# Short projections of a hybrid decoder's recurrence: float32 multiplications replaced by pairs of float32r multiplications on split rows

## The chip, the cores and the metric

One core of one Trainium2 chip runs the whole program. The metric is the device time of one launch in microseconds (us); less is better.

## The reference, cut to what matters

One layer of a decoder is computed for 264 columns: 256 tokens of a prompt and one new token for each of 8 decoded sequences. Its parts are a feed-forward half step, a mixer, an attention over 256 memory tokens and a second half step. The mixer has a recurrence of 16 heads of 64 and a convolution beside it; the lines that the change touches compute this part of the recurrence:

```python
r, k, v, wd, ad, gd = jnp.split(pm, SPLITS, axis=-1)       # pm: shifted projections
w_log = -softplus(-(w0 + tanh(wd) @ w2_decay)) - 0.5        # wd: 64 columns
decay = exp(-exp(w_log))
a = sigmoid(a0 + ad @ a2_iclr)                              # ad: 64 columns
g = sigmoid(gd) @ g2_gate                                   # gd: 160 columns
kk = (k * k_k).reshape(B, T, 16, 64)
kk = kk / maximum(norm(kk, axis=-1), 1e-12)                 # a sum by head
...                                                         # recurrence -> y
bonus = sum(r * k * r_k, axis=-1) * v                       # a sum by head
o_a = (group_norm(y) + bonus) * g                           # two more sums by head
merged = concat([o_a * beta_rwkv, o_b * beta_conv]) @ w_out
```

## The kernel before, in words

**Tiling.** Activations lie with features on partitions and the 264 columns along the free axis. Each large weight matrix comes from memory in tiles of 128 by 1024 (raw, 512 KB). ScalarE copies a tile to float32r (whi, L188), VectorE computes the rest (wlo, L189), and TensorE makes three float32r multiplications for each block: high weight by high activation, high by low, low by high (L303 to L305, result acc). This stream of tiles runs through the whole program. The loads stand in SyncE's queue (L266).

**The recurrence.** Its 8 blocks of 128 features are worked in four groups of two (groups 0 to 3), while the projections of the mixer stream: MIX_ORDER (L40) names which projection follows which, and generators (rw_state, rw_read, rw_out, with the decode rows and the convolution) are stepped in between. What a generator yields is a pace; the tile scheduler then sets each engine's order from its own costs. `lora` (L704) makes the short activations: wdad (64 rows of tanh(wd), 64 of ad) and sga, sgb (sigmoid(gd)). `rw_state` (L719) does for each group: loads the short weights w2a2 and g2 (L727 to L736, half filled with zeros by GpSimd), the squares of k (L746), two multiplications for the decay (pw, L749), two for a (pa, L761), the scan (L766), two sums of squares by head against the block of ones blk (ps, L772), Ln and Exp, and the operands ar, bk and q. The rows q for decode (L811 to L813) are transposed by TensorE (L1010). Then come the gram matrices (L886 on TensorE, G by L890 on VectorE), transposes of bk (L825), and the inversion of small triangles, which alternates TensorE (L843, L850) and VectorE (L835, L836, L851, L852). I call this the gram stretch. `rw_read` (L963) has the sum for the bonus (L977), `rw_out` (L1078) the two sums for the group norm (L1087, L1093) and the gate's multiplications (L1104, L1105), each with two per block.

**The end of the mixer.** `mixer_out` (L1274) splits the 16 blocks of the result into xh and xl (L189) and `out_proj` (L1206) multiplies them by w_out, beginning with block 0 in four accumulators; its first low part, xl of block 0, is a VectorE instruction.

Of the kernel before, what the change touches and what calls it, by code (L numbers as in the profile page):

```python
# [8 lines left out]
F32 = mybir.dt.float32  # L9
F32R = mybir.dt.float32r  # L10
# [11 lines left out]
T = TP + TB  # L22
# [31 lines left out]
class Builder:  # L54
# [553 lines left out]
    def mixer_consts(self):  # L608
# [23 lines left out]

        self.blk = self.ct([128, 128], "blk")
        nc.vector.memset(self.blk, 0.0)
        for o in HS:
            nc.vector.memset(self.blk[o, o], 1.0)

# [65 lines left out]

    def lora(self, P):  # L704
        nc = self.nc
        xh, xl = self.xs
        self.wdad, self.sga, self.sgb = (self.mt(n) for n in ("wdad", "sga", "sgb"))
        ((a0, a1),) = yield from self.gemm(P[0], xh, xl)
        self.shift(a0, 24, self.wdad)
        self.fn(self.wdad[0:64], self.wdad[0:64], AF.Tanh)  # L710
        self.shift(a1, 25, self.sga)
        self.fn(self.sga, self.sga, AF.Sigmoid)
        ((b0,),) = yield from self.gemm(P[1], xh, xl)
        self.shift(b0, 26, self.sgb)
        self.fn(self.sgb[96:128], self.sgb[96:128], AF.Sigmoid)


    def rw_state(self, g, S):
# [7 lines left out]

        w2a2, g2 = self.mt("w2a2", (128, 2, 256), bufs=2), self.mt("g2", (128, 2, 256), bufs=2)  # L727
        for n, o in enumerate(HS):
            nc.gpsimd.memset(w2a2[o, 1 - n], 0.0)
        nc.gpsimd.memset(g2[0:96, 1], 0.0)  # L730
        gs = slice(256 * g, 256 * g + 256)
        nc.sync.dma_start(w2a2[0:64, 0], self.I["w2_decay"][0][:, gs])
        nc.sync.dma_start(w2a2[64:128, 1], self.I["a2_iclr"][0][:, gs])
        nc.sync.dma_start(g2[:, 0], self.I["g2_gate"][0][0:128, gs])
        nc.sync.dma_start(g2[96:128, 1], self.I["g2_gate"][0][128:160, gs])
        S["g2"] = g2  # L736
        c8 = lambda t: t[:, :, :TP].rearrange("p i (c t) -> p i c t", t=C)
# [5 lines left out]
        a = S["a"] = self.mt("a", G3)  # L743
        t1, t2 = self.mt("t1", G3), self.mt("t2", G3)
        for i, j in enumerate(js):
            A.activation(t1[:, i], k[:, i], AF.Square, scale=self.mcol("k_k", j))  # L746
        pw = [self.misc() for _ in js]
        for i, j in enumerate(js):
            mm(pw[i][:, :T], w2a2[:, 0, cs[i]], self.wdad, start=True, stop=True)  # L749
        for i, j in enumerate(js):  # L750
# [9 lines left out]
        for i, j in enumerate(js):  # L760
            mm(pa[i][:, :T], w2a2[:, 1, cs[i]], self.wdad, start=True, stop=True)  # L761
        for i, j in enumerate(js):
            self.fn(a[:, i], pa[i][:, :T], AF.Sigmoid, bias=self.mcol("a0", j))
        L = self.mt("L", (128, NP, C + 1))
        fl = lambda t: t.rearrange("p c t -> p (c t)")
        V.tensor_tensor_scan(fl(L), fl(self.rst), fl(sig), 0.0, ALU.mult, ALU.add)  # L766
        Lc = sig
# [3 lines left out]
        for i, j in enumerate(js):  # L771
            mm(ps[i][:, :T], self.blk, t1[:, i], start=True, stop=True)  # L772
        for i, j in enumerate(js):
# [191 lines left out]
    def rw_read(self, g, S):  # L965
# [6 lines left out]
        for i, j in enumerate(js):  # L972
            V.scalar_tensor_tensor(r[:, i], r[:, i], self.mcol("r_k", j), k[:, i], ALU.mult, ALU.mult)
        yield 1.0
        for i, j in enumerate(js):
            p = self.misc()
            mm(p[:, :T], self.blk, r[:, i], start=True, stop=True)  # L977
            V.tensor_tensor(v[:, i], p[:, :T], v[:, i], ALU.mult)
# [25 lines left out]
    def decode_rows(self, g, S):  # L1004

        nc = self.nc
        q = S["q"]
        n = 5 * 2 * TB
        ps = self.misc()
        nc.tensor.transpose(ps[:n, :128], q[:, 0:5].rearrange("p q i b -> p (q i b)"), self.ident)  # L1010
        row = self.mt("row", (n, 128))
        nc.scalar.activation(row, ps[:n, :128], AF.Copy)
        self.rows[g] = scr = self.dram.tile([10, 2, TB, C], F32, tag="row", name=self.uid("scr"), bufs=4)
        for h in range(2):
            nc.scalar.dma_start(
                scr[:, h], row[:, C * h : C * h + C]
            )
# [61 lines left out]
    def rw_out(self, g, S):  # L1079
        nc = self.nc  # L1080
        V, A = nc.vector, nc.scalar
        mm = nc.tensor.matmul
        y, t1, t2, bon, g2 = S["y"], S["k"], S["r"], S["v"], S["g2"]
        js = (2 * g, 2 * g + 1)
        for i in range(2):
            p = self.misc()
            mm(p[:, :T], self.blk, y[:, i], start=True, stop=True)  # L1087
            V.scalar_tensor_tensor(y[:, i], p[:, :T], -1.0 / C, y[:, i], ALU.mult, ALU.add)
# [12 lines left out]
        for i, j in enumerate(js):  # L1101
            cs = slice(128 * i, 128 * i + 128)
            p = self.misc()
            mm(p[:, :T], g2[:, 0, cs], self.sga, start=True, stop=False)  # L1104
            mm(p[:, :T], g2[:, 1, cs], self.sgb, start=False, stop=True)  # L1105
            V.scalar_tensor_tensor(self.oa[j], y[:, i], self.mcol("beta_rwkv", j), p[:, :T], ALU.mult, ALU.mult)
# [144 lines left out]
    def mixer(self, pool, P):  # L1251
# [5 lines left out]
        self.last = self.mt("last", (128, 27, TB + 1))  # L1257
        self.rst = self.mt("rst", (128, NP, C + 1))
        nc.gpsimd.memset(self.rst, 1.0)
# [614 lines left out]
```

## Time and profile before

| | |
|---|---|
| median of 3 runs | 2525.59 us (2519.16 to 2527.02) |
| the profiled execution | 2526.33 us, of which the span is 2524.6 us |
| granted TensorE clock, mean | 0.993 |
| TensorE busy | 2470.9 us, 98% |
| VectorE busy | 1582.8 us, 63% |
| ScalarE busy | 1195.0 us, 47% |
| GpSimd busy | 261.7 us, 10% |

TensorE has work nearly all the time over the span. The shares are means over stages that differ: in the stretch of the recurrence VectorE's share is much higher than its 63%. Starts are counted from the start of the span. Matmuls overlap, so the distance from one start to the next says what one takes, not its length.

### The profile page before, as it was taken

To read this page: it belongs to the slowest core of one execution; us is meant where nothing else is said; L and a number is where in the kernel's file an instruction comes from. 1 tells how busy PE (TensorE), PEld (TensorE's weight loads), DVE (VectorE), ACT (ScalarE), POOL (GpSimd) and SP (SyncE) were. 2 spreads that over 40 slices of the span, in tenths; PEclk is the share of its full clock that TensorE was granted. 3 is DMA by queue.
4 is the path that set the end of the run, shared out by engine and by line. 5 is a ranking of instruction groups with operands and counts; after the bars stand their busy time and mean duration, and the time that the engine had idled before them with its cause. 6 is when DMAs were issued, how large, how long until landed. Compare 5 with 4: busy or idle time off the path is not lost. (4 is left out here: it accounts for less than half of the span.)

```text
span 2524.6 us, 53420 instructions
## 1 busy us (share of the span) xinstructions
PE 2470.9 (98%) x22328; PEld 2417.2 (96%) x22328; DVE 1582.8 (63%) x2545; ACT 1195.0 (47%) x1802; POOL 261.7 (10%) x422
## 2 busy tenths in 40 slices
PE   9999999999999999999989999999999999999998
PEld 9999999999999988988889888989999999999998
DVE  5545444444557599799777566789655545554465
ACT  5444433444446555455646354657444434444443
POOL 1300000000000001000110222220132500000000
PEclk9999999999999999999999999999999999999999
DMA  7656655555557754544476799976677755655554
GB/s 228 188 183 220 203 183 182 183 183 178 179 181 212 221 151 132 149 131 139 128 251 224 262 293 305 322 226 191 195 215 217 237 182 184 183 178 183 176 180 131
DMA packets 452211, 497.89 MB, mean 197 GB/s; under 512 B 22096, under 2 KB 418640, under 8 KB 451968
## 3 DMA queue, kind: packets, MB, share of 16 engines
q1 hardware_dynamic: 417840, 417.09, 54.0%
q0 software_dynamic: 20992, 67.22, 8.4%
q10 hardware_dynamic: 13136, 10.15, 1.2%
q8 instruction: 175, 2.87, 0.5%
q14 instruction: 68, 0.56, 0.1%
HBM read 477.76 MB, written 16.63 MB: 196 GB/s over the span
## 5 line engine op out<-in xcount | busy, mean ns | idle before, releaser
L189 DVE TENSOR_TENSOR wlo<-raw,whi 128x1024 fp32r<-128x1024 f32 (+1 forms) x791 | 961.4, 1216 | 850.6 <-ACT whi L188 847.3
L188 ACT ACTIVATE whi<-raw 128x1024 fp32r<-128x1024 f32 (+1 forms) x791 | 823.0, 1041 | 1035.6 <-PE acc L304 856.6
L303 PE MATMUL acc<-xh,whi 128*128 128x264 f32 x2864 | 828.7, 290 | 15.3 <-DVE y L1243 7.3
L304 PE MATMUL acc<-xl,whi 128*128 128x264 f32 x2864 | 820.2, 287 | 0.6 <-DVE xl L189 0.6
L305 PE MATMUL acc<-xh,wlo 128*128 128x264 f32 x2864 | 816.7, 286 | 0.5 <-DVE wlo L189 0.5
L303 PEld LDWEIGHTS acc<-xh,whi 128*128 128x128 f32 x2864 | 540.3, 189 | 23.8 <-ACT rh L1328 7.5
L304 PEld LDWEIGHTS acc<-xl,whi 128*128 128x128 f32 x2864 | 542.0, 189 | 3.7 <-DVE xl L189 0.8
L305 PEld LDWEIGHTS acc<-xh,wlo 128*128 128x128 f32 x2864 | 541.0, 189 | 2.3 <-DVE wlo L189 1.1
L303 PE MATMUL acc<-rh,whi 128*128 128x264 f32 (+2 forms) x1600 | 456.8, 285 | 0.2 <-ACT lnx L397 0.2
L305 PE MATMUL acc<-rh,wlo 128*128 128x264 f32 (+2 forms) x1600 | 454.5, 284 | 0.0
L304 PE MATMUL acc<-rl,whi 128*128 128x264 f32 (+2 forms) x1600 | 453.4, 283 | 0.0
L304 PE MATMUL acc<-gl,whi 128*128 128x264 f32 x1408 | 400.2, 284 | 0.0
L305 PE MATMUL acc<-gh,wlo 128*128 128x264 f32 x1408 | 400.1, 284 | 0.0
L303 PE MATMUL acc<-gh,whi 128*128 128x264 f32 x1408 | 399.5, 284 | 0.0
L303 PEld LDWEIGHTS acc<-rh,whi 128*128 128x128 f32 x1600 | 300.8, 188 | 2.2 <-ACT lnx L397 0.4
L304 PEld LDWEIGHTS acc<-rl,whi 128*128 128x128 f32 x1600 | 301.7, 189 | 1.2
L305 PEld LDWEIGHTS acc<-rh,wlo 128*128 128x128 f32 x1600 | 300.7, 188 | 0.2
L305 PEld LDWEIGHTS acc<-gh,wlo 128*128 128x128 f32 x1408 | 264.5, 188 | 0.1
L304 PEld LDWEIGHTS acc<-gl,whi 128*128 128x128 f32 x1408 | 264.5, 188 | 0.0
L303 PEld LDWEIGHTS acc<-gh,whi 128*128 128x128 f32 x1408 | 264.3, 188 | 0.1
L1176 DVE SCALAR_TENSOR_TENSOR y<-u,cw,y 128x256 f32<-128x256 f32 x240 | 111.1, 476 | 0.6
L397 ACT ACTIVATE lnx<-acc 128x264 f32<-128x264 f32 x84 | 32.4, 386 | 64.8 <-PE acc L305 64.8
(350 smaller groups left out, 2089.9 us busy)
## 6 DMA issues: line engine op xcount, KB each, us to landing
raw<-in_ffn_w SPq DMA_DIRECT2D x509, 512.0 KB, 3.6
raw<-in_w_in SPq DMA_DIRECT2D x86, 512.0 KB, 3.8
raw<-in_w_mk SPq DMA_DIRECT2D x32, 512.0 KB, 3.4
raw<-in_w_mv SPq DMA_DIRECT2D x32, 512.0 KB, 5.4
raw<-in_w_out SPq DMA_DIRECT2D x32, 512.0 KB, 5.1
kv<-in_cache_mem_k POOLq DMA_DIRECT2D x32, 512.0 KB, 6.2
raw<-in_w_mq SPq DMA_DIRECT2D x32, 512.0 KB, 5.2
kv<-in_cache_mem_v POOLq DMA_DIRECT2D x32, 512.0 KB, 6.1
```

The source lines that it names most:

```text
L188: a = self.nc.scalar.activation(hi, src, AF.Copy)
L189: return a, self.nc.vector.tensor_tensor(lo, src, hi.bitcast(F32), ALU.subtract)
L303: nc.tensor.matmul(out, wh, xh, start=start, stop=False)
L304: nc.tensor.matmul(out, wh, xl, start=False, stop=False)
L305: self.mark = nc.tensor.matmul(out, wl, xh, start=False, stop=stop)
L397: self.lastfn = self.nc.scalar.activation(*args, **kw)
L1176: V.scalar_tensor_tensor(c[:, :TP], u[:, i : i + TP], w(i), c[:, :TP], ALU.mult, ALU.add)
```

## The change

Every multiplication of pw, pa, ps, of the bonus sum and of the gate, which took float32 operands, now takes float32r operands whose activation is split into a high and a low part, so that one multiplication becomes two (pw, pa, ps, bonus) and the gate's two become four. The two sums of the group norm stay as they are. For w2a2 both parts of the weight stand on the array's 128 rows at once: the 64 rows of the weight are loaded twice, the high part above, the low part below, and the activation is copied to both halves. The last 32 rows of g2 are loaded four times in the same way. What this needs:

- in `lora` (once): 8 small copies from SBUF to SBUF in GpSimd's queue, three splits on VectorE and their copies on ScalarE;
- in each group, on ScalarE: copies of 128 by 528 for the squares and for the bonus row, and of 128 by 512 for w2a2 and for g2;
- in each group, on GpSimd: the subtractions for the low parts, two of 128 by 528 (L745), one of 64 by 512 (L764), one of 128 by 256 (L1127), two of 32 by 256 (L1129); three memsets go away;
- in each group, in SyncE's queue: 9 loads in place of 4, into a buffer (wraw) of which there is one, for both w2a2 and g2;
- the scan is in two halves, and the decode row's tile moves to another pool.

```diff
-        self.blk = self.ct([128, 128], "blk")
-        nc.vector.memset(self.blk, 0.0)
+        m = self.t1("lnx", bufs=4)[:, :128]
+        nc.vector.memset(m, 0.0)
         for o in HS:
-            nc.vector.memset(self.blk[o, o], 1.0)
+            nc.vector.memset(m[o, o], 1.0)
+        self.blkr = self.ct([128, 128], "blk", F32R)
+        nc.scalar.activation(self.blkr, m, AF.Copy)
+        self.blk = self.blkr.bitcast(F32)
...
-        self.wdad, self.sga, self.sgb = (self.mt(n) for n in ("wdad", "sga", "sgb"))
+        self.wah, self.wal = (self.mt(n, (128, 2, T), F32R) for n in ("wah", "wal"))
+        self.sgh, self.sgl, self.sgq = (self.mt(n, dt=F32R) for n in ("sgh", "sgl", "sgq"))
         ((a0, a1),) = yield from self.gemm(P[0], xh, xl)
-        self.shift(a0, 24, self.wdad)
-        self.fn(self.wdad[0:64], self.wdad[0:64], AF.Tanh)
-        self.shift(a1, 25, self.sga)
-        self.fn(self.sga, self.sga, AF.Sigmoid)
+        both, w = self.wal.bitcast(F32), self.t1("lnx", bufs=4)
+        self.shift(a0, 24, w)
+        self.fn(w[0:64], w[0:64], AF.Tanh)
+        for n, o in enumerate(HS):
+            for p in HS:
+                nc.gpsimd.dma_start(both[p, n], w[o])
+        w = self.t1("lnx", bufs=4)
+        self.shift(a1, 25, w)
+        self.fn(w, w, AF.Sigmoid)
+        self.split_from(w, self.sgh, self.sgl)
         ((b0,),) = yield from self.gemm(P[1], xh, xl)
-        self.shift(b0, 26, self.sgb)
-        self.fn(self.sgb[96:128], self.sgb[96:128], AF.Sigmoid)
+        self.split_from(both, self.wah, self.wal)
+        w, four = self.t1("lnx", bufs=4), self.t1("lnx", bufs=4)
+        self.shift(b0, 26, w)
+        self.fn(w[96:128], w[96:128], AF.Sigmoid)
+        for o in QS:
+            nc.gpsimd.dma_start(four[o], w[96:128])
+        A.activation(self.sgq, four, AF.Copy)
+        V.tensor_tensor(self.sgq[64:128], four[64:128], self.sgq[64:128].bitcast(F32), ALU.subtract)
+
+    def sums(self, p, hi, lo):
+
+        for n, x in enumerate((hi, lo)):
+            self.nc.tensor.matmul(p[:, :T], self.blkr, x, start=n == 0, stop=n == 1)
+
+    def split_rows(self, x, *tags):
+
+        hi, lo = (self.mt(t, (128, 1024 if t == "ar" else 2 * T), F32R)[:, : 2 * T].rearrange("p (i t) -> p i t", i=2) for t in tags)
+        self.nc.scalar.activation(hi, x, AF.Copy)
+        self.nc.gpsimd.tensor_tensor(lo, x, hi.bitcast(F32), ALU.subtract)
+        return hi, lo
...
-        w2a2, g2 = self.mt("w2a2", (128, 2, 256), bufs=2), self.mt("g2", (128, 2, 256), bufs=2)
-        for n, o in enumerate(HS):
-            nc.gpsimd.memset(w2a2[o, 1 - n], 0.0)
-        nc.gpsimd.memset(g2[0:96, 1], 0.0)
+        raw, w2a2 = self.mt("wraw", (128, 2, 256)), self.mt("w2a2", (128, 2, 256), F32R)
         gs = slice(256 * g, 256 * g + 256)
-        nc.sync.dma_start(w2a2[0:64, 0], self.I["w2_decay"][0][:, gs])
-        nc.sync.dma_start(w2a2[64:128, 1], self.I["a2_iclr"][0][:, gs])
-        nc.sync.dma_start(g2[:, 0], self.I["g2_gate"][0][0:128, gs])
-        nc.sync.dma_start(g2[96:128, 1], self.I["g2_gate"][0][128:160, gs])
-        S["g2"] = g2
+        for o in HS:
+            nc.sync.dma_start(raw[o, 0], self.I["w2_decay"][0][:, gs])
+            nc.sync.dma_start(raw[o, 1], self.I["a2_iclr"][0][:, gs])
+        A.activation(w2a2, raw, AF.Copy)
+        nc.gpsimd.tensor_tensor(w2a2[64:128], raw[64:128], w2a2[64:128].bitcast(F32), ALU.subtract)
...
+        sh, sl = self.split_rows(t1, "t2", "ar")
         pw = [self.misc() for _ in js]
         for i, j in enumerate(js):
-            mm(pw[i][:, :T], w2a2[:, 0, cs[i]], self.wdad, start=True, stop=True)
+            for n, x in enumerate((self.wah, self.wal)):
+                mm(pw[i][:, :T], w2a2[:, 0, cs[i]], x[:, 0], start=n == 0, stop=n == 1)
...
-            mm(pa[i][:, :T], w2a2[:, 1, cs[i]], self.wdad, start=True, stop=True)
+            for n, x in enumerate((self.wah, self.wal)):
+                mm(pa[i][:, :T], w2a2[:, 1, cs[i]], x[:, 1], start=n == 0, stop=n == 1)
...
-        V.tensor_tensor_scan(fl(L), fl(self.rst), fl(sig), 0.0, ALU.mult, ALU.add)
+        for i in range(2):
+            n = slice(NC * i, NC * i + NC)
+            V.tensor_tensor_scan(fl(L[:, n]), fl(self.rst), fl(sig[:, n]), 0.0, ALU.mult, ALU.add)
...
-            mm(ps[i][:, :T], self.blk, t1[:, i], start=True, stop=True)
+            self.sums(ps[i], sh[:, i], sl[:, i])
+        t2 = self.mt("t2", G3)
...
-        yield 1.0
+        sh, sl = self.split_rows(r, "t1", "t2")
+        yield 2.4
         for i, j in enumerate(js):
             p = self.misc()
-            mm(p[:, :T], self.blk, r[:, i], start=True, stop=True)
+            self.sums(p, sh[:, i], sl[:, i])
...
-        row = self.mt("row", (n, 128))
+        row = self.t1("lnx", bufs=4)[:n, :128]
...
-        y, t1, t2, bon, g2 = S["y"], S["k"], S["r"], S["v"], S["g2"]
+        y, t1, t2, bon = S["y"], S["k"], S["r"], S["v"]
         js = (2 * g, 2 * g + 1)
+
+        gr, gw, gl = self.mt("wraw", (128, 2, 256)), self.mt("g2", (128, 2, 256), F32R), self.mt("g2l", (128, 256), F32R)
+        gs = slice(256 * g, 256 * g + 256)
+        nc.sync.dma_start(gr[:, 0], self.I["g2_gate"][0][0:128, gs])
+        for o in QS:
+            nc.sync.dma_start(gr[o, 1], self.I["g2_gate"][0][128:160, gs])
+        A.activation(gw, gr, AF.Copy)
+        nc.gpsimd.tensor_tensor(gl, gr[:, 0], gw[:, 0].bitcast(F32), ALU.subtract)
+        for o in QS[1::2]:
+            nc.gpsimd.tensor_tensor(gw[o, 1], gr[o, 1], gw[o, 1].bitcast(F32), ALU.subtract)
         for i in range(2):
             p = self.misc()
             mm(p[:, :T], self.blk, y[:, i], start=True, stop=True)
@@ -1101,8 +1146,8 @@
         for i, j in enumerate(js):
             cs = slice(128 * i, 128 * i + 128)
             p = self.misc()
-            mm(p[:, :T], g2[:, 0, cs], self.sga, start=True, stop=False)
-            mm(p[:, :T], g2[:, 1, cs], self.sgb, start=False, stop=True)
+            for n, (w, x) in enumerate(((gw[:, 0], self.sgh), (gw[:, 0], self.sgl), (gl, self.sgh), (gw[:, 1], self.sgq))):
+                mm(p[:, :T], w[:, cs], x, start=n == 0, stop=n == 3)
```

**What moves on TensorE, at the inversion of group 3.** In these rows Q, G and P are the small triangles, mis is a scratch of PSUM, and acc is the weight stream. Before:

```order
L843 MATMUL mis_14916<-Q_14893,G_14821 32x32 [waits DVE_49,PE_49]
L843 MATMUL mis_14916<-Q_14893,G_14821 32x32 x31
L303 MATMUL acc_14795<-xh_9081,whi_14797 128x264
L304 MATMUL acc_14795<-xl_9097,whi_14797 128x264
L305 MATMUL acc_14795<-xh_9081,wlo_14798 128x264
L303 MATMUL acc_14796<-xh_9081,whi_14797 128x264
L850 MATMUL mis_14975<-P_14949,Q_14893 32x32 [waits Activation_49]
L850 MATMUL mis_14975<-P_14949,Q_14893 32x32 x31
L304 MATMUL acc_14796<-xl_9097,whi_14797 128x264
L305 MATMUL acc_14796<-xh_9081,wlo_14798 128x264
```

After:

```order
L884 MATMUL mis_15147<-P_15117,Q_15061 32x32 [waits Activation_49]
L884 MATMUL mis_15147<-P_15117,Q_15061 32x32 x31
L303 MATMUL acc_15232<-xh_15198,whi_14959 128x264 [waits DVE_49]
L877 MATMUL mis_15286<-Q_15061,G_14989 32x32 [waits DVE_49]
L877 MATMUL mis_15286<-Q_15061,G_14989 32x32 x31
L884 MATMUL mis_15360<-P_15319,Q_15061 32x32 [waits DVE_49,Activation_49]
L884 MATMUL mis_15360<-P_15319,Q_15061 32x32 x19
L303 MATMUL acc_15233<-xh_15198,whi_14959 128x264 [waits DVE_49]
L884 MATMUL mis_15360<-P_15319,Q_15061 32x32 x12
L304 MATMUL acc_15230<-xl_15214,whi_14959 128x264 [waits DVE_49]
```

Before, the stream of the last projection stands between the steps of the inversion. Now that projection has ended, the multiplications in between are single starts of out_proj's accumulators, and the first L304 of out_proj, which takes the low part xl_15214, comes directly behind. Between the q transpose of group 3 and this L304 there are 7 multiplications of the stream (3 of the last projection, 4 of out_proj); before, the stream's multiplications between the q transpose and the end of the second L850 are 55.

**What moves on VectorE, at the same place.** xl is the low part of block 0; the STT on y with cw is the convolution, v the shift of the last projection. Before:

```order
L835 COPY_PREDICATED Q_14893<-lm,G_14821 32x8x32
L1176 SCALAR_TENSOR_TENSOR y_9738<-u_14294,cw,y_9738 128x256
L836 STREAM_TRANSPOSE Q_14893<-Q_14893 128x8x32 [waits DVE_49]
L1176 SCALAR_TENSOR_TENSOR y_9738<-u_14294,cw,y_9738 128x256 [waits DVE_49]
L189 TENSOR_TENSOR xl_15121<-y_9723,xh_15105 128x264
L1176 SCALAR_TENSOR_TENSOR y_9738<-u_14294,cw,y_9738 128x256 [waits DVE_49]
```

After:

```order
L886 STREAM_TRANSPOSE Q_15061<-Q_15061 128x8x32 [waits DVE_49]
L1221 SCALAR_TENSOR_TENSOR y_9740<-u_14375,cw,y_9740 128x256 [waits DVE_49]
L705 SCALAR_TENSOR_TENSOR v_15188<-sst,mv,v_15188 128x8
L1221 SCALAR_TENSOR_TENSOR y_9740<-u_14375,cw,y_9740 128x256 [waits DVE_49]
L704 SCALAR_TENSOR_TENSOR v_15188<-acc_14891,mv,v_15188 128x255 [waits Activation_49]
L1221 SCALAR_TENSOR_TENSOR y_9740<-u_14375,cw,y_9740 128x256 [waits DVE_49]
L705 SCALAR_TENSOR_TENSOR v_15188<-sst,mv,v_15188 128x8
L189 TENSOR_TENSOR wlo_15235<-raw_14963,whi_15234 128x1024 [waits DMAHW7_49,Activation_49]
L189 TENSOR_TENSOR xl_15214<-y_9725,xh_15198 128x264
```

Before, xl of block 0 stands behind the first transpose of Q (L836). Now it stands behind the second one (L886, numbered by the changed file), the shifts of v and one more weight split. In the changed order 31 instructions stand ahead of it from the ar of group 3 (L851) on: ar itself, 4 G, 5 copies by mask, 2 transposes, 3 splits wlo, 12 of the convolution, and 4 shifts of v (two of 255 columns, two of 8).

The positions of the q transposes move too. Counted in multiplications of the stream that stand ahead of them: 7312, 7779, 8277 and 8738 before; 7322, 7809, 8304 and 8781 now.

## Rows read from the trace of the kernel before

**Rows 1.** Engines' busy times over the recurrence's stretch of the mixer, 870 to 1270 us after the span's start. Columns: the stretch, its length, the busy us of each engine with its instructions, the granted TensorE clock, the share of the DMA engines, GB/s.

```profile
870.00:1270.00 400.00, 384.06 (x5433) 351.00 (x5431) 350.01 (x772) 218.41 (x420) 40.23 (x83) 0.99 0.51 143
```

**Rows 2.** TensorE's waits between 870 and 1270 us: line, releaser, us in total, number, the longest. The names in it: q is the table of rows for decode, G and Q belong to the gram stretch.

```profile
PE mis L1010 <- DVE q L811: 3.5, 4, 2.0
PE mis L843 <- DVE Q L836: 3.2, 4, 1.2
PE mis L825 <- DVE G L890: 3.0, 4, 1.1
```

**Rows 3.** The timeline of TensorE at the gate of group 1: start in us, length in us (the ends are modelled), line, operands, count.

```profile
985.55 0.29 PE L305 MATMUL acc<-xh,wlo 128*128 128x264 f32 x1
985.68 0.61 PE L1104 MATMUL mis<-sga,g 128*128 128x264 f32 x2
986.12 0.61 PE L1105 MATMUL mis<-sgb,g 128*128 128x264 f32 x2
986.57 0.61 PE L1104 MATMUL mis<-sga,g 128*128 128x264 f32 x2
987.01 0.61 PE L1105 MATMUL mis<-sgb,g 128*128 128x264 f32 x2
987.26 0.48 PE L303 MATMUL acc<-xh,whi 128*128 128x264 f32 x1
987.58 0.29 PE L304 MATMUL acc<-xl,whi 128*128 128x264 f32 x1
```

**Rows 4.** Groups of TensorE's short multiplications between 860 and 1275 us, by shape: count, busy us and mean ns of one, idle time before. Each multiplication of the program is two records here.

```profile
L749 PE MATMUL mis<-wdad,w2a 128*128 128x264 f32 x16 | 4.5, 405 | 0.0
L772 PE MATMUL mis<-t,blk 128*128 128x264 f32 x16 | 4.2, 385 | 0.0
L1104 PE MATMUL mis<-sga,g 128*128 128x264 f32 x16 | 4.9, 386 | 0.0
```

**Rows 5.** VectorE's busy time in the stretches that end with the q rows of groups 0 to 3 (L811 stands at 903.00, 996.87, 1091.99 and 1185.35).

```profile
880.00:903.00 23.00, 23.00 (x51) 1.00 0.47 127
970.00:997.00 27.00, 26.34 (x60) 1.00 0.36 97
1060.00:1092.00 32.00, 30.31 (x71) 1.00 0.34 90
1170.00:1185.60 15.60, 15.38 (x36) 1.00 0.21 67
```

**Rows 6.** VectorE's timeline from just behind the q rows of group 3 on: start, length, line, operands. The distance between two starts is what an instruction costs on this engine.

```profile
1185.60 0.69 DVE L817 TENSOR_TENSOR ar<-r,L 128x512 f32<-128x512 f32 x1
1186.20 1.22 DVE L189 TENSOR_TENSOR wlo<-raw,whi 128x1024 fp32r<-128x1024 f32 x1
1187.34 0.48 DVE L1176 SCALAR_TENSOR_TENSOR y<-u,cw,y 128x256 f32<-128x256 f32 x1
1187.74 1.22 DVE L189 TENSOR_TENSOR wlo<-raw,whi 128x1024 fp32r<-128x1024 f32 x1
1188.87 2.48 DVE L890 TENSOR_TENSOR G<-mis,gmask 128x512 f32<-128x512 f32 x4
1191.27 1.80 DVE L835 COPY_PREDICATED Q<-lm,G 32x256 f32<-32x256 int32 x4
1193.09 0.49 DVE L1176 SCALAR_TENSOR_TENSOR y<-u,cw,y 128x256 f32<-128x256 f32 x1
```

**Rows 7.** All engines between those q rows and the second start of L850, and TensorE's groups of the weight stream in the same stretch.

```profile
1185.60:1201.10 15.50, 13.81 (x325) 12.13 (x329) 15.43 (x35) 5.46 (x12) 5.32 (x10) 1.00 0.68 217
L305 PE MATMUL acc<-xh,wlo 128*128 128x264 f32 x19 | 5.7, 297 | 0.0
L303 PE MATMUL acc<-xh,whi 128*128 128x264 f32 x18 | 5.4, 303 | 0.1
L304 PE MATMUL acc<-xl,whi 128*128 128x264 f32 x18 | 5.2, 289 | 0.0
```

**Rows 8.** GpSimd's multiplications and additions of 128 by 512 in the decode state (group, whole run), and one of them on GpSimd's timeline.

```profile
L1070 POOL TENSOR_TENSOR st<-st,dbc 128x512 f32<-128x512 f32 x8 | 12.9, 1614 | 27.1 <-DMA st<-in_wkv 27.1
L1071 POOL TENSOR_TENSOR dbc<-dbc,sa 128x512 f32<-128x512 f32 x8 | 9.1, 1142 | 38.2 <-DMA dbc<-scr 38.2
1815.69 2.16 POOL L1072 TENSOR_TENSOR st<-st,dbc 128x512 f32<-128x512 f32 x1
1818.39 1.29 POOL L1075 TENSOR_TENSOR st<-st,dbc 128x512 f32<-128x512 f32 x1
```

**Rows 9.** VectorE's timeline at the same time: the split of a weight tile (wlo) before, beside and beside these two.

```profile
1812.25 1.23 DVE L189 TENSOR_TENSOR wlo<-raw,whi 128x1024 fp32r<-128x1024 f32 x1 [1.00 <-ACT whi L188]
1815.17 1.53 DVE L189 TENSOR_TENSOR wlo<-raw,whi 128x1024 fp32r<-128x1024 f32 x1 [1.69 <-ACT whi L188]
1818.08 2.69 DVE L189 TENSOR_TENSOR wlo<-raw,whi 128x1024 fp32r<-128x1024 f32 x1 [1.39 <-ACT whi L188]
```

**Rows 10.** One line of VectorE in the attention's first steps, over all its 16 instructions: shortest, median and longest in ns, first and last start.

```profile
L446 DVE SCALAR_TENSOR_TENSOR rl<-y,lnv,rh x16: 476/484/1378, 1699.7 to 1738.8; 128x264 fp32r<-128x264 f32 x16
```

**Rows 11.** Waits of SyncE's queue of weight loads (L266) between 870 and 1270 us: what they wait for most (us in total, number, the longest).

```profile
SPq L266 <- DVE y L1176: 152.8, 38, 9.8
```

**Rows 12.** ScalarE between 860 and 1275 us: a table function on 128 by 528.

```profile
L397 ACT ACTIVATE t<-t 128x528 f32<-128x528 f32 x8 | 5.1, 637 | 2.0 <-DVE t L774 1.9
```

**Rows 13.** TensorE's granted clock behind the q rows of group 2.

```profile
1100.00:1120.00 20.00, 17.39 (x521) 15.94 (x522) 16.23 (x36) 5.94 (x10) 1.45 (x3) 0.83 0.50 130
```

More of the change, by code (lines that the diff above doesn't have):

```diff
@@ L705, in lora @@
         nc = self.nc
+        A, V = nc.scalar, nc.vector
         xh, xl = self.xs
-        self.wdad, self.sga, self.sgb = (self.mt(n) for n in ("wdad", "sga", "sgb"))
+        self.wah, self.wal = (self.mt(n, (128, 2, T), F32R) for n in ("wah", "wal"))
+        self.sgh, self.sgl, self.sgq = (self.mt(n, dt=F32R) for n in ("sgh", "sgl", "sgq"))
         ((a0, a1),) = yield from self.gemm(P[0], xh, xl)
-        self.shift(a0, 24, self.wdad)
-        self.fn(self.wdad[0:64], self.wdad[0:64], AF.Tanh)
-        self.shift(a1, 25, self.sga)
-        self.fn(self.sga, self.sga, AF.Sigmoid)
-        ((b0,),) = yield from self.gemm(P[1], xh, xl)
-        self.shift(b0, 26, self.sgb)
-        self.fn(self.sgb[96:128], self.sgb[96:128], AF.Sigmoid)
+        both, w = self.wal.bitcast(F32), self.t1("lnx", bufs=4)
[8 more added lines that the diff above has]
+        self.split_from(w, self.sgh, self.sgl)
+        ((b0,),) = yield from self.gemm(P[1], xh, xl)
+        self.split_from(both, self.wah, self.wal)
[14 more added lines that the diff above has]
+        return hi, lo
     def rw_state(self, g, S):
@@ L743, in rw_state @@
         a = S["a"] = self.mt("a", G3)
-        t1, t2 = self.mt("t1", G3), self.mt("t2", G3)
+        t1 = self.mt("t1", G3)
         for i, j in enumerate(js):
             A.activation(t1[:, i], k[:, i], AF.Square, scale=self.mcol("k_k", j))
+        sh, sl = self.split_rows(t1, "t2", "ar")
         pw = [self.misc() for _ in js]
         for i, j in enumerate(js):
-            mm(pw[i][:, :T], w2a2[:, 0, cs[i]], self.wdad, start=True, stop=True)
+            for n, x in enumerate((self.wah, self.wal)):
+                mm(pw[i][:, :T], w2a2[:, 0, cs[i]], x[:, 0], start=n == 0, stop=n == 1)
         for i, j in enumerate(js):
@@ L1257, in mixer @@
         self.last = self.mt("last", (128, 27, TB + 1))
-        self.rst = self.mt("rst", (128, NP, C + 1))
+        self.rst = self.mt("rst", (128, NC, C + 1))
         nc.gpsimd.memset(self.rst, 1.0)
```

## The prediction

> **What bounds the kernel now.** I read the engines' shares first: TensorE is at work 98% of the span, so its time can be sold for time only where it is what ends last. The change touches one stage, the mixer's recurrence, so next come the stage's own shares: of 400 us TensorE is busy 384.06 and VectorE 350.01, far more than VectorE's share of the whole [rows 1]. The waits of TensorE say where the 16 us are lost: three of its waits are for VectorE, all at the four gram stretches: 3.5 us for q, 3.2 for Q and 3.0 for G [rows 2]. Just ahead of each of the four q rows VectorE has hardly a gap: 23.00 of 23.00 us, 26.34 of 27, 30.31 of 32, 15.38 of 15.6 [rows 5]. So the stage has two bounds in turn: TensorE's stream between the gram stretches, VectorE at them. What is taken off TensorE ahead of such a place is worth nothing unless VectorE comes earlier too.
>
> **What it takes off TensorE.** In the gate of group 1 the two float32 multiplications of two blocks begin at 985.68 and the fifth start, a multiplication of the stream, is at 987.26, but what follows it only at 987.58; neighbours in the stream are 0.12 apart (985.55 to 985.68, [rows 3]). So four float32 multiplications take 987.58 − 985.68 − 0.12 = 1.78 us, 0.445 each (985.68, 986.12, 986.57, 987.01 say the same). A float32r multiplication of the same 264 columns takes 0.121. The other groups have the same shape and like records, 405 and 385 ns beside the gate's 386 [rows 4]. In each group of blocks:
> - pw, pa, ps and bonus: 8 times 0.445 becomes 16 times 0.121: 3.56 to 1.94, −1.62 us;
> - the gate: 4 times 0.445 becomes 8 times 0.121: 1.78 to 0.97, −0.81 us.
>
> That is −2.43 a group, **−9.7 us in all**. It is the most that this part can give: 0.39% of the time, when 0.3% (7.6 us) is about what a measurement of this kernel can tell from no change.
>
> **Where TensorE's saving can be spent.** The orders show that much of it is already spent: ahead of the four q transposes stand 10, 30, 27 and 43 more multiplications of the stream than before, work that stood in the gram stretches. At 0.121 that is 1.2, 3.6, 3.3 and 5.2 us. What TensorE saves up to the same places is 1.2 (pw, pa, ps of one group: 6 × 0.203), 3.6, 6.1 and 8.5. So it gets to q of groups 0 and 1 as before, to group 2 2.8 us earlier and to group 3 **3.3 us earlier**, if VectorE lets it. Behind the last q 1.2 us of saving are left (bonus and gate of group 3).
>
> **What VectorE and GpSimd get.** VectorE's own work hardly changes: a scan in halves, and once three splits in `lora`, ahead of the stretches that count; nothing for these. What could slow it are GpSimd's subtractions. Before, GpSimd does no arithmetic with tensors here, so the price is bounded from other stages. One of 128 by 512 takes 1.14 to 1.61 us on GpSimd [rows 8]. Beside one, a weight split that takes 1.23 us alone took 1.53, beside another 2.69 [rows 9]; a line of 0.484 us (median) took up to 1.378 [rows 10]. The excess is 0.30, 1.46 and 0.89 us, 0.9 in the mean, about the time of the subtraction itself at most; the other bound is nothing, where VectorE has a gap. About ten such subtractions (four for the squares, three for the bonus, three of w2a2) stand ahead of the last q. Half of them at 0.9 us makes 4.5 us of VectorE in its tight stretches; I take 4.3, with 0 and ten whole ones (11 to 16 us) as ends. So q of group 3 comes 4.3 − 3.3 = **+1.0 us**.
>
> The Trainium skill, SBUF — State Buffer, "SBUF: two separate sides", says that VectorE and GpSimd share a pair of ports under an exclusive lock held for the whole instruction, that a VectorE instruction with two inputs in SBUF takes part in it, and that the loser blocks fully. The row with 2.69 us agrees, the one with 1.53 shows that the loser can be GpSimd (its step there took 2.16 us). By that rule, as a forecast, every one of the ten would cost VectorE its own time; that is the second rival.
>
> **The seam to out_proj.** This is the term that the diff does not show. From the ar of group 3 on, VectorE has 31 instructions before the low part of out_proj's block 0: ar 0.60, 12 of the convolution at 0.40, 3 splits at 1.14, 4 G at 0.60, 4 copies by mask at 0.455, and 7 short ones (transposes, a copy, v) at 0.40 or less [rows 6]: 0.6 + 4.8 + 3.4 + 2.4 + 1.8 + at most 2.8 = 15.8, say 15.5 us. In the same 15.5 us before, TensorE did 55 multiplications of the stream and was busy 13.81 us [rows 7]; now it has 7 to do, and must idle some 7.5 us (13.81 − 48 × 0.121 = 8.0 busy) in place of 1.7. But those 48 were mostly done ahead of it: at its end the stream stands at 8781 + 7 = 8788 against 8738 + 55 = 8793 before. Five multiplications are **+0.6 us**.
>
> **The rest.** ScalarE gets four copies a group of about 0.64 us (its 128 by 528 takes 637 ns, [rows 12]), 2.5 us beside 218.41 busy of 400 [rows 1]: nothing, with 0.6 a group as upper end where the copy of the squares stands in the chain to q. The chain itself gets longer by that copy and a subtraction (0.64 + 1.2 to 1.7), but the multiplications ps stand over 5 us behind the squares in the order, which covers it. SyncE's five more loads a group and the one buffer wraw hold loads of the weight stream behind a split on GpSimd. That queue waits for VectorE's conversions anyway, 152.8 us in 38 waits behind the convolution alone [rows 11], so loads are early: nothing, at most about 1 us a group. Three memsets fewer on GpSimd: nothing.
>
> **The sum.** The profiled execution took 2526.33 us. +1.0 (q of group 3), +0.6 (seam), −1.2 (bonus and gate behind it) make 2526.7. It stands 0.74 above the median of the runs; against that median I forecast **2526 us**, no change that can be told. Of −9.7 us nearly all goes: 5.2 into multiplications put ahead of q, which come back as idle time at the seam, 4.3 into VectorE.
>
> **Rivals.**
> 1. *The saving lands.* VectorE follows TensorE (GpSimd's steps fall into its gaps), and waits of before go: −3.3 + 0.6 − 1.2 = −3.9, with the 3.5 us for q gone too −7.4, and −9.7 or a little more if the stretch of reduced clock behind group 2 (0.83 over 20 us, [rows 13]) also goes, 3.4 us. That is 2516 to 2519. For it: VectorE has 50 us of gaps in 400. Against it: they do not lie ahead of q [rows 5]. Chance 0.19.
> 2. *Slower: GpSimd takes VectorE's time.* All ten subtractions fall into the full stretches and each costs its 1.14 to 1.61 us: 11 to 16 us, less 3.3, so q of group 3 comes 8 to 13 us late and the total is +7 to +12: 2533 to 2538. It decides from about 11 us of added VectorE time. For it: the row with 2.69, and that most of VectorE's instructions ahead of q read two inputs in SBUF. Against it: 1.53, and that the steps for w2a2 are made a group ahead. Chance 0.19.
> 3. *The weight stream is held* behind wraw, 1 us a group and a ScalarE copy of 0.6 in the chain: +6 with the forecast's own, 2533. Against it: the queue's slack [rows 11]. Chance 0.05.
> 4. *The multiplications don't get faster*: if float32r on these rows cost what float32 does, 48 more times 0.445, +21 us. The stream's own 0.121 speaks against it. Chance 0.02.
>
> **How the numbers follow.** My forecast, everything between −7 and +7, has 0.55; faster by over 0.3% is the first rival, 0.19; slower the other three, 0.26. The range takes the first rival in nearly whole and the second to its end: 2515 to 2538.
>
> **What would show it.** Right: TensorE busy about 10 us less and idle about as much more; 7 to 8 us idle between the q transpose of group 3 and the first L304 of out_proj, released by xl; weight splits of 1.5 to 2.7 us beside GpSimd's subtractions; q waits longer than before. Wrong: q of group 3 more than 4 us earlier or 5 later against the start of the mixer; new waits for wraw or DMAs on TensorE; multiplications of the short weights further apart than 0.12.

## The result, and the profile after

| | before | after |
|---|---|---|
| median | 2525.08 us (2519.16 to 2527.02) | 2554.81 us (2553.70 to 2556.05) |
| ratio | | 1.0128 (95% interval 1.0114 to 1.0143) |
| profiled execution | 2526.33 us, span 2524.6 | 2556.05 us, span 2554.3 |
| mean granted clock | 0.993 | 0.986 |

The change makes the kernel 30 us slower. I had forecast 2526 us and a range up to 2538.

The page first. TensorE has 10 us less to do and is busy 5 us longer than before (2470.9), and idle 78.0 us where it was 53.7:

```profile
PE 2476.3 (97%) x22328; PEld 2423.8 (95%) x22328; DVE 1594.6 (62%) x2552; ACT 1202.4 (47%) x1822; POOL 296.8 (12%) x442
```

So the 29.7 us are +24.3 of idle time, −9.7 of work saved, and some 15 us of work made longer. That fits the granted clock: 0.95 in place of 0.99 over the 400 us of the stage is, as an estimate, some 16 us. The same stretch as in [rows 1]:

```profile
870.00:1270.00 400.00, 361.68 (x5205) 333.14 (x5203) 350.49 (x746) 213.97 (x418) 65.61 (x89) 0.95 0.48 139
```

VectorE is busy in it as long as before (350.49 us, with 746 instructions for 772), TensorE only 361.68 in place of 384.06, at a clock of 0.95. TensorE's waits there, as in [rows 2] (L884, L877 and L859 are the former L850, L843 and L825; P is ScalarE's copy between two steps of the inversion), with the row on P of the kernel before as the last:

```profile
PE mis L884 <- ACT P L879: 11.2, 7, 3.5
PE mis L877 <- DVE Q L870: 6.2, 4, 4.1
PE mis L1045 <- DVE q L845: 3.9, 4, 1.5
PE mis L884 <- issue: 3.4, 1, 3.4
PE mis L859 <- DVE G L924: 3.4, 4, 1.1
PE mis L877 <- issue: 2.5, 1, 2.5
```

```profile
PE mis L850 <- ACT P L845: 1.1, 1, 1.1
```

q and G have changed little (3.5 and 3.0 before); Q has gone from 3.2 to 6.2 us, of which 4.1 is one wait at the seam. New is P: 11.2 us for 1.1. ScalarE was late. Group 1's gram stretch shows why. ScalarE there (start, length, line, operands, idle time before and what ended it):

```profile
1007.89 1.06 ACT L188 ACTIVATE whi<-raw 128x1024 fp32r<-128x1024 f32 x1
1008.86 0.62 ACT L763 ACTIVATE w2a<-wraw 128x512 fp32r<-128x512 f32 x1
...
1017.45 1.06 ACT L188 ACTIVATE whi<-raw 128x1024 fp32r<-128x1024 f32 x1 [4.77 <-DMA raw<-in_w_in]
1018.42 1.25 ACT L860 ACTIVATE bkT<-mis,sign 128x512 f32<-128x512 f32 x2
1021.27 0.63 ACT L1126 ACTIVATE g<-wraw 128x512 fp32r<-128x512 f32 x1 [1.61 <-DMA wraw<-in_g_gate]
...
1023.60 0.40 ACT L879 ACTIVATE P<-mis 128x256 f32<-128x256 f32 x1
1032.14 1.06 ACT L188 ACTIVATE whi<-raw 128x1024 fp32r<-128x1024 f32 x1 [8.14 <-DMA raw<-in_w_in]
1033.10 0.37 ACT L879 ACTIVATE P<-mis 128x256 f32<-128x256 f32 x1
```

It works in order. At 1017.45 it had waited 4.77 us for a tile of the weight stream (raw), at 1032.14 another 8.14, and bkT and P stood behind. SyncE's queue in the same stretch:

```profile
1000.89 0.37 SPq L266 DMA_DIRECT2D raw<-in_w_in  x1
1012.00 0.34 SPq L1123 DMA_DIRECT2D wraw<-in_g_gate  x1
...
1013.72 0.39 SPq L266 DMA_DIRECT2D raw<-in_w_in  x1
...
1014.76 0.50 SPq L266 DMA_DIRECT2D raw<-in_w_in  x1
1015.31 0.49 SPq L1125 DMA_DIRECT2D wraw<-in_g_gate  x1
1025.54 0.48 SPq L761 DMA_DIRECT2D wraw<-in_w_decay  x1
...
1028.15 1.08 SPq L266 DMA_DIRECT2D raw<-in_w_in  x2
```

Between 1000.89 and 1013.72, and again between 1014.76 and 1028.15, no tile of the stream is asked for: the loads of the short weights stand ahead and wait for the buffer wraw. And GpSimd, whose subtractions free it:

```profile
1009.61 2.36 POOL L764 TENSOR_TENSOR w2a<-wraw,w2a 64x512 fp32r<-64x512 f32 x1 [1.94 <-ACT w2a L763]
...
1022.04 0.93 POOL L1127 TENSOR_TENSOR g2l<-wraw,g 128x256 fp32r<-128x256 f32 x1 [1.45 <-PE mis L877]
1023.06 2.46 POOL L1129 TENSOR_TENSOR g<-wraw,g 32x256 fp32r<-32x256 f32 x2
```

The load at 1012.00 comes when L764 ends, the one at 1025.54 when L1129 ends. Over the stage ScalarE's waits for the stream are 23.7 us in four (us in total, number, longest), where the kernel before has 5.0 in two (the second row); behind them three of SyncE's waits at the loads into wraw:

```profile
ACT whi L188 <- DMA raw<-in_w_in: 23.7, 4, 8.1
ACT whi L188 <- DMA raw<-in_w_in: 5.0, 2, 4.3
SPq L1123 <- POOL w2a L764: 14.5, 2, 10.7
SPq L761 <- DMA wraw<-in_g_gate: 8.8, 2, 5.4
SPq L1123 <- POOL sig L769: 5.9, 1, 5.9
```

In `lora` the first loads of wraw do the same to ScalarE directly; its copy waits 3.05 us, the projection's accumulators are emptied late (lnx), and TensorE waits:

```profile
838.61 0.63 ACT L763 ACTIVATE w2a<-wraw 128x512 fp32r<-128x512 f32 x1 [3.05 <-DMA wraw<-in_a_iclr]
...
847.78 0.64 ACT L188 ACTIVATE wah<-wal 128x528 fp32r<-128x528 f32 x1 [4.25 <-DMA wal<-lnx]
PE acc L303 <- DVE lnx L704: 4.4, 1, 4.4
```

### The profile page after: what moved, and what is told of

It reads as the page before. It is cut to its first block, busy times and chain, and to the rows that moved or that the text cites. A ratio compares the mean times of both kernels' runs of the same rounds, so it can differ in the third digit from the quotient of the medians.

```text
span 2554.3 us, 53531 instructions
## 1 busy us (share of the span) xinstructions
PE 2476.3 (97%) x22328; PEld 2423.8 (95%) x22328; DVE 1594.6 (62%) x2552; ACT 1202.4 (47%) x1822; POOL 296.8 (12%) x442
## 4 chain that ended last, share of the span: by engine, by line
PE 84%; DMA 6%; DVE 4%; issue 3%; ACT 2%; POOL 1%; SPq 0%; POOLq 0%; ACTq 0%; DVEq 0%
PE acc L303 26%; PE acc L305 26%; PE acc L304 26%; DVE wlo L189 1%; ACT whi L188 1%; DMA raw<-in_w_mv 1%; DMA raw<-in_ffn_w 1%; DVE y L1221 1%; DMA raw<-in_w_mq 1%; DMA raw<-in_w_mo 1%; DMA kv<-in_cache_mem_v 0%; PE mis L1502 0%; PE mis L884 0%; DMA raw<-in_w_mk 0%; PE mis L1517 0%
## 5 line engine op out<-in xcount | busy, mean ns | idle before, releaser
L304 PE MATMUL acc<-xl,whi 128*128 128x264 f32 x2864 | 824.9, 288 | 1.2 <-DVE xl L189 1.2
L304 PEld LDWEIGHTS acc<-xl,whi 128*128 128x128 f32 x2864 | 546.7, 191 | 3.6 <-DVE xl L189 1.6
L304 PE MATMUL acc<-rl,whi 128*128 128x264 f32 (+2 forms) x1600 | 454.0, 284 | 0.0
L304 PE MATMUL acc<-gl,whi 128*128 128x264 f32 x1408 | 400.2, 284 | 0.0
L304 PEld LDWEIGHTS acc<-rl,whi 128*128 128x128 f32 x1600 | 301.8, 189 | 1.2
L304 PEld LDWEIGHTS acc<-gl,whi 128*128 128x128 f32 x1408 | 264.5, 188 | 0.0
L1221 DVE SCALAR_TENSOR_TENSOR y<-u,cw,y 128x256 f32<-128x256 f32 x240 | 118.3, 502 | 0.4
```

What stands on the lines that cost most here:

```text
L304: nc.tensor.matmul(out, wh, xl, start=False, stop=False)
L1221: V.scalar_tensor_tensor(c[:, :TP], u[:, i : i + TP], w(i), c[:, :TP], ALU.mult, ALU.add)
```

## The experiments

Ratios are to the kernel before on the same chip, with 95% intervals; 0.1% is 2.5 us. Three theories of the loss are tested: "A", the weight stream is held by wraw; "B", GpSimd takes VectorE's time; "C", the copies in `lora`. Waits and positions come from one profiled execution of each kernel.

**Where the loads, the copies and the low parts are made (e1 to e5).** e1: all loads into wraw become `nc.gpsimd.dma_start`.

> The short weights' loads (9 a group, into wraw) leave SyncE's queue and go into GpSimd's; all else as in the change. Theory A (the one buffer wraw makes SyncE's queue wait, and the loads of the weight stream behind it come late in each gram stretch; ScalarE waits in order for such a load, so P and TensorE come late too): ScalarE's waits for raw fall from 23.7 us to about 6, TensorE's waits for P from 11.2 to about 2, and the time falls by 12 to 20 us, to 2535 to 2543. Theory B (GpSimd's subtractions take VectorE's time): no change, 2550 to 2557. Theory C (the small copies in lora): no change either.

Measured 1.0091 (1.0064 to 1.0117). ScalarE's wait for raw fell from 23.7 to 5.7 us, as A says, but the time fell only 9 us (0.37% of 2525), less than the 12 to 20 that A expected, and its interval just touches that of the change. Part of the rest may be ScalarE's waits for wraw's own late loads, 9.8 us where the change had 4.3:

```profile
ACT whi L188 <- DMA raw<-in_w_in: 5.7, 2, 3.8
ACT g L1126 <- DMA wraw<-in_g_gate: 9.8, 2, 5.9
```

e2: `dma_start(both[p, n], w[o])` becomes `V.tensor_copy(b[p], w[o])` with a split of each half behind it, and the same for `four`.

> The 8 small SBUF to SBUF copies of lora are made by VectorE instead of DMAs (through two more short tiles, so that ScalarE never waits for a DMA there); all else as in the change. Theory C: ScalarE's wait of 4.25 us for these copies and TensorE's wait of 4.4 us behind it go, with the reduced clock that follows: -5 to -7 us, 2548 to 2550, and everything after 870 us as in the change. Theories A and B: these waits are hidden by what comes later, no change, 2553 to 2556.

1.0127 (1.0101 to 1.0153): nothing. TensorE still waited 3.3 us for lnx, since ScalarE's wait for wraw (now 3.90 us) stands ahead of it. C fell; what the rest of `lora` costs is not priced by this run.

> Both edits at once: the short loads in GpSimd's queue and lora's copies on VectorE. Theories A and C together: -18 to -26 us, 2529 to 2537, thus near the kernel before. Theory B: at most the 5 to 7 us of lora, 2548 or more.

1.0077 (1.0052 to 1.0102). That is not told apart from e1, and lies between the two expectations.

e4: `gpsimd.tensor_tensor` becomes `vector.tensor_tensor` in all low parts.

> All low parts of the short operands are subtracted by VectorE instead of GpSimd; loads and lora as in the change. VectorE gets some 3 us of work more a group, GpSimd's 5 to 9 us a group go. Theory B (GpSimd's subtractions block VectorE): 8 to 15 us faster, 2540 to 2547. Theory A: the buffer wraw is freed by VectorE in place of GpSimd, at times later, the weight stream is held as before: 2550 to 2560.

1.0035 (1.0023 to 1.0047): 23 us of the 30 gone by moving work onto the busier engine. That is more than B's 8 to 15, and A had expected none; raw's waits also fell, to 14.0 us. So it doesn't tell A from B.

> Three edits at once: low parts on VectorE, short loads in GpSimd's queue, lora's copies on VectorE. If the three costs add (e1 took off 7, e4 21, e2 nothing alone): 2524 to 2529, ScalarE's waits for raw back at about 6 us. If e4 had already taken the weight stream's hold away with it, and GpSimd's arithmetic was the whole cost: 2531 to 2536, as e4. Theory of the seam: even so no gain against the kernel before, for TensorE still idles 6 to 8 us between the q transpose of group 3 and the first low part of out_proj.

1.0033 (1.0006 to 1.0061), as e4 alone. ScalarE's waits for raw are still 13.0 us, though no load into wraw stands in SyncE's queue any more: wraw isn't the only thing that holds the stream.

**Which low parts (e9, e10).** e9 moves only these:

```diff
-        nc.gpsimd.tensor_tensor(w2a2[64:128], raw[64:128], ...)
+        V.tensor_tensor(w2a2[64:128], raw[64:128], ...)
-        nc.gpsimd.tensor_tensor(gl, gr[:, 0], ...)        # and gw[o, 1]
+        V.tensor_tensor(gl, gr[:, 0], ...)
```

> Of the change's low parts only those of the short weights (w2a2 and g2, 4 steps a group, the ones that hold the buffer wraw) go from GpSimd to VectorE; the low parts of the squares and of the bonus row stay on GpSimd. Theory A (GpSimd's queue holds wraw, wraw holds SyncE's queue and with it the weight stream): most of e4's 21 us, 2536 to 2543, ScalarE's waits for raw down from 23.7 us to about 14 as in e4. Theory B (GpSimd's arithmetic blocks VectorE, and the long subtractions of 128 by 528 do so most): a third or less, 2546 to 2553.

e10 moves only the one in `split_rows`.

> The complement: the low parts of the squares and of the bonus row (2 steps of 128 by 528 a group) go to VectorE, those of the short weights stay on GpSimd. Theory A: little, 2548 to 2556, the waits for raw stay near 24 us. Theory B: most of e4's 21 us, 2536 to 2543.

e9 1.0049 (1.0034 to 1.0064), e10 1.0107 (1.0081 to 1.0133). Moving the four short steps that free wraw gave back 20 us, moving the two long ones some 5 (its interval overlaps that of the change). In e9 the queue's longest wait for the short steps is 5.0 us (10.7 in the change), and ScalarE's waits for raw are 8.9 us on w_in and 4.7 on w_out:

```profile
SPq L1123 <- DVE g L1129: 5.0, 1, 5.0
SPq L1123 <- DVE w2a L764: 3.9, 2, 3.1
ACT whi L188 <- DMA raw<-in_w_in: 8.9, 3, 3.1
ACT whi L188 <- DMA raw<-in_w_out: 4.7, 2, 4.5
```

B could hide in this, since the same edit takes GpSimd's steps from VectorE's side. The traces weigh it. In the change, VectorE's instructions beside the short steps took 7.2 us longer in total than the medians of the same forms in kernels without these steps. In e9 VectorE makes the 16 steps itself, 4 of 0.69 and 12 of 0.42 us, 7.8 us. Its time is about the same either way, so the 20 us are not VectorE's time: GpSimd as the slow holder of wraw is shown as the larger part of the loss. Of it e1 gives 9 us to the weight stream alone; how the rest divides is not shown, and no run gave wraw a second buffer. e10 can't price B for the same reason: VectorE lost 5.7 us beside the long steps and pays 5.6 for making them.

**Parts of the change (e6, e7, e12).** e6 is the kernel before with `split_rows` and `sums` at ps and the bonus alone, e12 the same on VectorE, e7 the change with these two back in float32.

> The kernel before with the two sums by head (squares of k, bonus) in float32r alone, low parts on GpSimd as in the change: no short weights, no wraw, no copies in lora. TensorE saves 16 times 0.203 = 3.2 us. GpSimd's arithmetic as the cost (8 subtractions of 128 by 528): +3 to +9 against before, 2526 to 2532. The weight stream's hold and lora as the cost: -3 to 0, 2520 to 2523.

> e6 (the two sums by head alone) with its low parts on VectorE. Saves 3.2 us on TensorE. GpSimd's arithmetic as e6's cost: 2 to 4 us faster than e6, 2520 to 2523. VectorE as the bound ahead of q (its 8 added steps of 0.65 us): the same as e6 or up to 4 slower, 2524 to 2529.

> The change with the two sums back in float32: short weights and gate in float32r, wraw, lora and the loads as in the change. TensorE saves 6.5 us. The weight stream's hold as the cost: nearly the whole loss stays, 2540 to 2552, ScalarE's waits for raw near 24 us. GpSimd's arithmetic as the cost (its 4 steps a group are shorter): about half stays, 2533 to 2540.

e6 1.0004 (0.9990 to 1.0019), e12 1.0018 (1.0001 to 1.0035), e7 1.0066 (1.0045 to 1.0088). The sums alone gain nothing, and cost nothing with GpSimd; with VectorE they cost some 4 us, at the edge of what can be told. The projections are half of the loss. In e7 A missed: it expected raw's waits near 24 us, and they were 10.0, with wraw's loads and short steps as in the change.

```profile
ACT whi L188 <- DMA raw<-in_w_in: 10.0, 3, 6.8
```

So the hold is long only with the sums' steps beside it, which share GpSimd's and ScalarE's queues with the short ones. That would explain why the two parts do not add up to 1.0128; it is argued, not shown.

**Paces (e8, e11).** e8 sets HEAD_PACE to 0.8 in e5, e11 CONV_PACE.

> e5 with the recurrence's steps paced at 0.8 in place of 1.0: in the order the q transpose of group 3 stands 16 multiplications of the stream earlier, its inversion as before at the seam. Theory of the seam (VectorE ends last there, the place of TensorE's instructions alone doesn't matter): within 3 us of e5. If the order of TensorE's stream sets the loss: 2 to 5 us faster than e5.

> e5 with the convolution's steps paced at 0.8 in place of 1.0: in the order 6 multiplications of the stream stand between the q transpose of group 3 and its first inversion step as before, but 40 and 64 more ahead of the next steps, since out_proj's first low part no longer waits behind the whole convolution. Theory of the seam (it costs e5 some 8 us: idle time and the clock reduced behind it): 4 to 8 us faster than e5's 2534, 2526 to 2530. If the seam is no cost of its own: 2532 to 2537.

e8 1.0062 (1.0042 to 1.0081), e11 1.0115 (1.0078 to 1.0152). Both missed, on the slow side. In e11 raw's waits were 28.0 us in ten, and SyncE's queue waited 172.9 us for buffers that VectorE's splits free, 126.5 in e5. More VectorE work ahead of the stream's splits would do that; it is my reading, not shown by a run.

**The seam's clock (e13, e14).** In `rw_state` of group 3 of e9 (e13) and of e5 (e14), `mm(p, self.ident, ar...)` stands ten times between the steps, its result unread.

> e9 with ten useless float32 multiplications of ar (128 by 512, some 0.87 us each, result not read) put between the steps of group 3's inversion, where TensorE idled 6.9 us before out_proj. They give nothing but activity. If the clock that falls to half behind that idle time (13.7 us at 1198 to 1212 and 6.8 at 1222, about 10 us of TensorE's work lost) is the seam's cost: 5 to 9 us faster than e9, 2526 to 2530. If the seam costs by the idle time alone, which stays whatever TensorE does: the same or up to 3 us slower, 2535 to 2538.

> e5 with the same ten multiplications. Clock as the seam's cost: 5 to 9 us faster than e5, 2525 to 2529, level with the kernel before. Idle time alone: 2534 to 2537.

The same stretch in e9 and then in e13 (the column behind POOL is the granted clock):

```profile
1198.00:1213.00 15.00, 10.60 (x284) 9.59 (x285) 13.49 (x33) 3.21 (x7) 6.17 (x12) 0.54 0.57 178
```

```profile
1198.00:1213.00 15.00, 14.08 (x236) 8.46 (x235) 14.93 (x35) 4.45 (x8) 6.32 (x12) 1.00 0.57 188
```

The clock stayed at 2.4 GHz instead of falling to 1.2, and the time did not answer: 1.0044 (1.0029 to 1.0059) for e9's 1.0049, 1.0035 (1.0022 to 1.0047) for e5's 1.0033. VectorE is busy 13.49 and 14.93 of these 15 us, so I read it as VectorE ending last there. The runs don't show what the half clock costs by itself, for the useless multiplications take TensorE's time too: it is busy 14.08 us with 236 instructions, where it was 10.60 with 284.

**VectorE relieved (e15 to e17).** `if i % 3:` ahead of the convolution's step leaves out 10 of its 30 steps (its result is then incomplete), in the kernel before, in e5 and in the change.

> The kernel before with 10 of the convolution's 30 steps left out in each tile (80 steps of 0.40 us, 32 us of VectorE; the convolution's result is incomplete). VectorE as the pace of the stage: 3 to 8 us faster than before (the waits at the gram stretches and what the clock loses there), 2516 to 2521. TensorE as the only bound: within 2 us of before.

> e5 with the same steps left out. VectorE as the pace: TensorE's saving lands, 3 to 9 us faster than e15. If the loss lies in loads and in ScalarE's queue: it stays 5 to 10 us slower than e15, as e5 is slower than before.

> The change with the same steps left out. The weight stream held by wraw as the main loss: 8 to 20 us slower than e15, since room on VectorE does not bring the loads earlier. VectorE, blocked by GpSimd, as the main loss: 0 to 5 us slower than e15 or faster.

0.9996 (0.9981 to 1.0010), 1.0006 (0.9991 to 1.0022), 1.0043 (1.0027 to 1.0059). The kernel before gains nothing from 32 us less on VectorE, e5 gains 7, the change 21, and the change's waits for raw fall to 11.1 us. So two things make the hold: wraw's long turn, and a VectorE that has no room to catch up when a tile comes late. e16's expectation missed: it is level with e15, so TensorE's saving does not appear even then.

## Why the prediction was wrong, point by point

- **TensorE's saving** by the piece was right. The gate's float32r multiplications stand 0.12 us apart, as [rows 3] has for the stream:

```profile
997.89 0.29 PE L1150 MATMUL mis<-sgh,g 128*128 128x264 f32 x1
998.01 0.28 PE L1150 MATMUL mis<-sgl,g 128*128 128x264 f32 x1
998.14 0.28 PE L1150 MATMUL mis<-sgh,g2l 128*128 128x264 f32 x1
```

- **That the saving would not come back** came out, but the reason given, that VectorE ends last ahead of q, is not enough to explain it. e15 has 32 us less on VectorE and its q of group 3 6.9 us earlier (1178.47), yet the attention's first load comes only 2.2 us earlier (1353.12) and the time is that of before. An earlier q there was mostly lost again behind it, while the sum carries q's place into the time one to one. The q rows, from the timelines (L811 before, L845 in the change), and the first load of in_w_mq, the attention's first weight, in SyncE's queue:

| group | before | change | e4 | e9 | e6 |
|---|---|---|---|---|---|
| 0 | 903.00 | 911.45 | 904.15 | 909.13 | 903.23 |
| 1 | 996.87 | 1010.75 | 999.95 | 1004.76 | 996.94 |
| 2 | 1091.99 | 1112.48 | 1094.55 | 1097.42 | 1092.64 |
| 3 | 1185.35 | 1208.88 | 1190.61 | 1191.90 | 1184.87 |
| in_w_mq | 1355.28 | 1384.83 | 1366.82 | 1367.28 | 1355.96 |

In e4 and e6, with the hold smaller or absent, the distances from group to group are those of before within 3 us, though TensorE saves 2.4 (e4) or 0.8 us a group. **q of group 3 at +1.0 us was the sum that failed: +23.5.** The prediction named "5 later" as what would prove it wrong.

- **The step that failed** is the one on SyncE's queue: "so loads are early: nothing, at most about 1 us a group". I read from [rows 11] that the queue waits for VectorE anyway, and took its waiting for slack. It is the opposite: this queue, waiting for buffers, asks for each tile at the last moment, and a load put in front of a tile that waits for something else delays the stream by its own wait (10.7 us the longest). ScalarE's waits for raw went from 5.0 to 23.7 us. The loads alone are worth 9 us (e1), with the holder's steps 20, 5 a group (e9). I had also named the holder and not counted its time: ScalarE's copy, then GpSimd's 1.3 to 2.4 us, behind what stands in GpSimd's queue. As rival 3 it had a chance of 0.05 and +6.

- **`lora` at nothing** was wrong too. q of group 0 came 8.45 us late, with 4.4 us of TensorE's wait for lnx and a reduced clock behind it (0.91 from 840 to 860): ScalarE's w2a2 copy, put ahead of the projection's copies, waited for its loads. I had counted `lora`'s splits on VectorE and not its DMAs and ScalarE's order.

- **VectorE beside GpSimd**: I took 4.3 us, from 0 to 16. The mechanism shows, down to the q row itself, 0.17 us before and now 1.26, beside a step that took 2.36 (the group of these steps is 1.29 at its shortest); further on a step of the convolution of 1.53, where the median is 0.475:

```profile
1009.61 1.21 DVE L189 TENSOR_TENSOR wlo<-raw,whi 128x1024 fp32r<-128x1024 f32 x1
1010.75 1.26 DVE L845 TENSOR_TENSOR q<-q,r 128x16 f32<-128x16 f32 x1
1092.75 1.53 DVE L1221 SCALAR_TENSOR_TENSOR y<-u,cw,y 128x256 f32<-128x256 f32 x1
```

The size was too small: ahead of the last q VectorE's instructions beside GpSimd's lost some 12 us, within the 11 to 16 of rival 2. The count of ten subtractions had left out the gate's three short ones a group; 20 stood ahead of that q. Whether these 12 us cost time is not shown, since e9 and e10 give VectorE as much work as they spare it. The Trainium skill, SBUF — State Buffer, "SBUF: two separate sides", says that whichever of the two starts first holds the shared ports for its whole instruction and the other fully blocks. The trace agrees: beside the split of 1.21 us at 1009.61 GpSimd's step took 1.07 longer than its shortest, and the q row then took 1.09 longer than before and ended with that step.

- **The chain to ps.** I took the copy and the subtraction ahead of it as covered by the order. TensorE waited 1.5 us in one piece for the low part of the squares (ar, L745) in the change, so it was covered in most groups and not in all.

- **The seam** idled as worked out. From the q transpose (1209.19) to the first L304 of out_proj TensorE idled 6.6 us in 16.8 (I had 7.5 in 15.5), released by xl:

```profile
1209.20:1226.00 16.80, 10.19 (x306) 8.41 (x307) 16.55 (x36) 5.25 (x13) 6.72 (x10) 0.71 0.55 153
1209.19 0.28 PE L1045 MATMUL mis<-ident,q 128*80 128x128 f32 x1 [0.42 <-DVE q L845]
1218.18 1.08 PE L877 MATMUL mis<-Q,G 32*32 32x32 f32 x64 [4.05 <-DVE Q L870]
...
1225.43 0.59 PE L304 MATMUL acc<-xl,whi 128*128 128x264 f32 x1 [0.64 <-DVE xl L189]
```

Not foreseen was the clock, 0.71 over it; e13 kept it up and gained nothing. And the price behind q was wrong: the sum had −0.6 us there (+0.6 for the seam, −1.2 for bonus and gate), and from q of group 3 to the first load of in_w_mq the change takes 6.0 us longer than before. e4 takes 6.3 longer and e9 5.4, about half of the 11.5 and 12.0 us by which that load still comes late in them. (The profiled executions of e4, e9 and e16 lie 6 to 8 us above the medians of their kernels, so a part of their distances is noise.) Which instruction costs it stays open; the granted clock there was 0.75 from 1220 to 1240 and 0.83 from 1240 to 1260.

- **Left open**: where TensorE's 10 us go in e5 and e16, with the loads out of SyncE's queue and, in e16, VectorE relieved. The traces hint at a part: in e16 q of group 0 stands at 906.20 and in e15 at 899.29, 6.9 us later, with 3.8 us of TensorE's waits for lnx in `lora` ahead of it, and the first load of in_w_mq is 6.8 us later too. The inversion is a chain of short steps between three engines, whose length TensorE's saving does not touch; that is argued, not shown. No kernel run here is clear of noise faster than the one before.

## What to carry to other kernels

The queue here, always waiting for its buffers, had no slack: before you put another load into such a queue, ask what that load waits for and how long its buffer is held, and count the holder's whole chain. Here small loads with one buffer and a slow engine at its end cost more than the matrix work they serve saved. And where an engine is busy 98% because it always finds something to fill in, taking work off it need not gain time. Here it did not even with the next engine relieved (e16): follow one checkpoint behind another to the end before a term goes into the sum.

## What the runs showed of the hardware

- Steps of VectorE and GpSimd that both read SBUF ran one after the other: 1.21 us of weight split, then GpSimd's step (2.36 us from its start, 1.29 at the shortest), then a 0.17 us instruction of VectorE that took 1.26. The 24 subtractions on GpSimd lengthened VectorE's instructions beside them by 12.9 us in total.
- TensorE's clock fell to 1.2 GHz (half) for nearly all of the 15 us from 1215 on (0.54 in the mean), after it had idled 4.05 us in one piece; in e13 useless multiplications in the like gap kept it at 2.4 GHz (1.00 granted, 0.54 in e9), and the time stayed the same within the interval.
